# A two-layer attention trunk: the first half of layer one's output projection in pairs of tokens by 512 columns

## The chip, the cores and the metric

One core of one Trainium2 chip runs the whole kernel. The metric is the device time of one execution in microseconds (us), lower is better. Where a time is that of several runs, it is their median.

## What is computed

The trunk has two layers on 512 tokens by 1024 channels in float32. Layer one is a sparse-attention mixer of three branches (compressed, selected, sliding window), layer two a differential attention. The change lies in the last step of layer one, `o @ w_out`:

```python
    o = gate[..., 0:1] * o_c + gate[..., 1:2] * o_s + gate[..., 2:3] * o_w
    o = o.astype(u.dtype).reshape(b, s, NSA_WIDTH) * jax.nn.silu(z)
    return o @ w_out
...
        x = x + rmsnorm(y, norm_post[i])
```

`o` has 512 tokens by 1024 channels (16 heads of 64), `w_out` is 1024 by 1024.

## The kernel before

**Products.** A float32 product is made from three products of rounded parts: activations and weights are each split into a rounded value (`hi`, on ScalarE, L99) and the remainder (`lo`, on VectorE, L104), and `hi*hi`, `hi*lo` and `lo*hi` are added up in a PSUM bank. In the projection this is `mm` (L481): a 128 by 128 block of the attention output (128 channels, the k-chunk, by 128 tokens) is loaded into TensorE as the held operand, and columns of `w_out` stream past it. The attention output lies transposed in bigF (`oT`, 8 chunks of 128 channels by 512 tokens), its two parts in bigA and bigB (`U["oh"]`, `U["ol"]`). The names in the trace follow: `whi`/`wlo` are the two parts of a weight piece, `mm`, `S`, `T` and `av` are PSUM banks (two, two, three and one of them).

**Weights.** All weights of the program come as one stream of pieces (`ws`). A piece is loaded by SP's queue into one of two raw buffers (`wraw`, L125) and split by `ws.split()` into one of three pairs of buffers (`whi`, `wlo`). As a rule POOL does both parts (L170, L172). The "quick" pieces around the projection are rounded on ScalarE (L168), and their remainders go by turns to VectorE and POOL (L172). The three "extra" pieces of the second half are loaded into `P` tiles (L121), of which there are eleven and which the softmaxes use as well, and split into `wx`. A split of the next piece is asked for at the end of each piece's use; its load follows when a raw buffer is free.

**The first half of the projection** (`ojobs` with `early`). Output columns 0 to 511 are made while the attention still runs. Job oA makes columns 0 to 255 of all four tiles of 128 tokens from k-chunks 0 to 5, in the two `mm` banks, with two tokens' 256 columns in each bank. Job oB does the same for columns 256 to 511 in the two `S` banks. Each has weight pieces of 4 and 2 chunks by 256 columns. Job oC (`late_run`) adds chunks 6 and 7 to all of them when the last heads are done, and ends each tile and half with `y_evac` (L467, L468: a square sum on ScalarE, a product with the norm's weight on VectorE). Then job o1 makes columns 512 to 1023, 512 at a time, from four pieces that are all held.

**The order of the work.** The attention of the last group of heads is written as units (scores and softmax in `a`, transposes in `t`, products with V in `v`; L888 is the product with V). oA is spread over the last slots of that loop. After the loop come the remaining `t` and `v` calls, and after each of them two steps of oB (`fill`, `OB = (2,2,2)`); a step is a yield of `early_run`, three matmuls. The last unit is the compressed branch (`Cmp`): its `t` makes the transposed probabilities and the masked V (L980), its two `v` calls have three products each (L989 to L991) and add them to chunks 6 and 7 (L993). Then `fill(99)` writes out the rest of oB:

```python
    fill(99)
    for c, e in ((6, getattr(nc, ZE[0])), (7, getattr(nc, ZE[1]))):
        e.tensor_tensor(oT[:, c, :], oT[:, c, :], T["z", c], op=OP.mult)
    for c in (6, 7):
        osplit(c)
```

The multiplication by z (L1089) of chunk 6 is on POOL, of chunk 7 on VectorE; `osplit` makes the two parts. oC, o1 and the first jobs of layer two follow in an order written by hand. The rest is put in order by a scheduler that simulates a timeline; each engine then takes its instructions in the order that comes out.

Of the kernel before, what the change touches and what calls it, by code (L numbers as in the profile page):

```python
# [18 lines left out]
S = 512  # L19
# [35 lines left out]
D = 1024  # L55
NT = S // 128
# [11 lines left out]
def trunk(ctx: ExitStack, tc: tile.TileContext, x, table, npre, npost, w_in, pe_k, w1_k, w2_k,  # L68
# [11 lines left out]
    def bank(tag):  # L80
        return ps.tile([128, 512], F32, name=tag, tag=tag, bufs={"mm": 2, "S": 2, "T": 3, "av": 1}[tag])

    def slot(tag, shape, dt=F32):
        return big.tile(shape, dt, name="big" + tag, tag="big" + tag)
# [4 lines left out]
    def pttile(dt=F32R):  # L89
        return work.tile([128, 512], dt, name="PT", tag="PT", bufs=NPT)  # L90

    def small(n, dt=F32, tag="st", bufs=8):
        return work.tile([128, n], dt, name=tag, tag=tag, bufs=bufs)

    def drows(src, off, ap):
        return bass.AP(tensor=src.tensor, offset=src.offset + off, ap=ap)
# [81 lines left out]
    T = {}  # L178
    todo = []
    ws = Stream()  # L180
    U = {}

    def wcols(w, width, col, n, k0=0, nk=KD):
        return (lambda a, m: drows(w, (k0 + a) * 128 * width + col, [[width, 128], [128 * width, m], [1, n]])), nk, n
# [159 lines left out]
    def part_sum(ss, m=EPS):  # L344

        m0 = small(1, tag="m0", bufs=6)
        if isinstance(m, float):
            nc.vector.tensor_scalar(m0, ss, 1.0 / D, m, op0=OP.mult, op1=OP.add)
        else:
            nc.vector.scalar_tensor_tensor(m0, ss, 1.0 / D, m, op0=OP.mult, op1=OP.add)  # L350
        return m0
# [112 lines left out]
    def y_evac(t, p, a, n, last):  # L464
        c = slice(a, a + n)
        ss = small(1, tag="ss")
        nc.scalar.activation(pttile(F32)[:, :n], p, AF.Square, accum_out=ss)  # L467
        nc.vector.tensor_tensor(T["y"][:, t, c], p, T["gp"][a // 512][:, a % 512:a % 512 + n], op=OP.mult)  # L468
        if last:
            T["yend"](t, ss)  # L470
        else:
            T["ym", t] = part_sum(ss, T.get(("ym", t), EPS))

    def ojobs(name, w, early):


        specs = [[wcols(w, D, n * 512, 512, 2 * i, 2) for i in range(4)] for n in range(2)]

        def mm(p, t, k, wt, start, stop):
            for j, (wi, u) in enumerate(((0, "oh"), (1, "oh"), (0, "ol"))):  # L480
                nc.tensor.matmul(p, U[u][:, k, t * 128:(t + 1) * 128], wt[wi],  # L481
                                 start=start and j == 0, stop=stop and j == 2, skip_group_check=True)

        def run0(i):
            ps_ = [bank(b) for b in ("mm", "S", "mm", "S")]
            for c in range(4):
                h, l = ws.cut.pop(i + c)
                for t in range(NT):
                    for k in range(2):
                        mm(ps_[t], t, 2 * c + k, (h[:, k], l[:, k]), c == 0 and k == 0, c == 3 and k == 1)  # L490
                        yield 640.0
                    if c == 3:
                        y_evac(t, ps_[t], 0, 512, False)
                ws.split()

        def run1(i):
            for _ in range(2):
                ws.split()
            cut = [ws.cut.pop(i + c) for c in range(4)]
            for t in range(NT):  # L500
                parts = 1 if early or t < NT - 1 else 2
                n = 512 // parts
                for q in range(parts):
                    p = bank(("mm", "S")[(t + q) % 2])[:, :n]
                    for k in range(KD):
                        h, l = (v[:, k % 2, q * n:q * n + n] for v in cut[k // 2])
                        mm(p, t, k, (h, l), k == 0, k == KD - 1)
                        yield 640.0 / parts
                    y_evac(t, p, 512 + q * n, n, q == parts - 1)
            ws.split()  # L510
            ws.split()

        def early_run(q):
            def run(i):
                T["ob", q] = [bank(("mm", "S")[q]) for _ in range(2)]
                for c in range(2):
                    h, l = ws.cut.pop(i + c)
                    for k in range((4, 2)[c]):
                        if q == 0 and todo and todo[0] == 4 * c + k:
                            osplit(todo.pop(0))  # L520
                        for t in range(NT):
                            mm(T["ob", q][t // 2][:, t % 2 * 256:t % 2 * 256 + 256], t, 4 * c + k, (h[:, k], l[:, k]),
                               c == 0 and k == 0 and t % 2 == 0, False)
                            yield 320.0
                    ws.split()
            return run

        def late_run(i):
            h, l = ws.cut.pop(i)
            for t0 in (0, 2):  # L530
                for q in range(2):
                    c = slice(q * 256, q * 256 + 256)
                    for t in (t0, t0 + 1):
                        for k in range(2):
                            mm(T["ob", q][t // 2][:, t % 2 * 256:t % 2 * 256 + 256], t, 6 + k, (h[:, k, c], l[:, k, c]),
                               False, k == 1)
                            yield 320.0
                for t in (t0, t0 + 1):
                    for q in range(2):
                        y_evac(t, T["ob", q][t // 2][:, t % 2 * 256:t % 2 * 256 + 256], q * 256, 256, False)  # L540
            ws.split()

        if early:
            for q in range(2):
                Job(name + "AB"[q], [wcols(w, D, q * 256, 256, 0, 4), wcols(w, D, q * 256, 256, 4, 2)], early_run(q),
                    24 * 320.0)
            Job(name + "C", [wcols(w, D, 0, 512, 6, 2)], late_run, 16 * 320.0)
        else:
            Job(name + "0", specs[0], run0, 8 * 4 * 640.0)
        j = Job(name + "1", specs[1], run1, 8 * 4 * 640.0)  # L550
        ws.extra |= set(range(j.first + 1, j.first + 4))
        ws.quick |= set(range(j.first - (QN if early else 4), j.first + 4))
# [31 lines left out]
    for c in (4, 5, 6, 7):  # L584
        zjob(c)
    ojobs("o", w_out, True)


# [29 lines left out]
    dqk(6), dqk(7)  # L618
    dz(6), dz(7)
    ojobs("do", dw_out, False)  # L620
    index = {j.name: i for i, j in enumerate(jobs)}
    ws.extra.add(jobs[index['dv1']].first)
# [91 lines left out]
    for i, key in enumerate(("kcs", "vcs")):  # L714

        t = slot("CD"[i], [128, 5, 8, 33])
# [283 lines left out]
    def osplit(c):  # L1000
        hi(U["oh"][:, c], oT[:, c])
        lo(U["ol"][:, c], oT[:, c], U["oh"][:, c])
# [72 lines left out]
    i = 0  # L1075
# [265 lines left out]
```

## Time and profile before

| | |
|---|---|
| Runs shown, us | 646.47, 646.88, 647.7 (median 646.88) |
| Profiled execution, us | 647.41 |
| Its span, first to last instruction, us | 645.6 |
| Mean granted clock of TensorE | 0.997 |
| TensorE busy | 629.6 us, 98% of the span, 3447 matmuls |
| VectorE, ScalarE, POOL busy | 62%, 53%, 62% |
| Chain that ended last | TensorE 84%, VectorE 7%, ScalarE 4% |
| DMA | 59.94 MB, 93 GB/s over the span |

In the timelines that the prediction reads, a row is: start in us, duration in us, engine, line, operation, output <- inputs, shape, count, and in brackets the idle time of the engine just before and what ended it. Rows of TensorE have a modelled end, so the spacing is read from start to start. PEld is the loading of the held operand, SPq the issue of a DMA on SP's queue.

### The profile page before, as it was taken

The numbers are of one execution on the slowest core, as the hardware profiler recorded it, in microseconds if no ns is written. First come the engines' busy times: TensorE is split into PE (matmuls) and PEld (weight loads), VectorE is DVE, ScalarE is ACT, GpSimd is POOL, SyncE is SP. The second block draws the span as 40 slices with busy tenths as digits, with TensorE's granted clock in tenths as the row PEclk, the third lists the DMA queues.
The fourth block names the chain that finished last, engine by engine and source line by source line (L and its number), as shares of the span: only waits on it lengthen the run. The fifth ranks groups of instructions, "written<-read, shape, count | busy, mean of one in ns | idle before, by whom it ended". The sixth has DMA issues, their size and how long they took to land.

```text
span 645.6 us, 10462 instructions
## 1 busy us (share of the span) xinstructions
PE 629.6 (98%) x3447; PEld 534.1 (83%) x3447; DVE 397.4 (62%) x1142; ACT 342.7 (53%) x902; POOL 402.0 (62%) x663
## 2 busy tenths in 40 slices
PE   8999999999999999999999999999999999999996
PEld 5988888888788888888888898888888888878785
DVE  5421335678768868979777800245657767787544
ACT  7221234767667777868555410344574466677331
POOL 5558668878588596678485657865666555514200
PEclk9999999999999999999999999999999999999998
DMA  7646423214022111101953132423222322117102
GB/s 252 165 104 160 130 81 87 63 35 98 2 66 64 36 48 52 49 17 35 304 165 126 66 98 66 130 70 111 80 69 82 82 67 70 61 66 266 61 34 97
DMA packets 71915, 59.94 MB, mean 93 GB/s; under 512 B 3613, under 2 KB 62901, under 8 KB 71862
## 3 DMA queue, kind: packets, MB, share of 16 engines
q1 hardware_dynamic: 71140, 56.93, 30.2%
q10 hardware_dynamic: 722, 2.36, 0.9%
q8 instruction: 27, 0.44, 0.3%
q14 instruction: 26, 0.21, 0.1%
HBM read 54.52 MB, written 4.76 MB: 92 GB/s over the span
## 4 chain that ended last, share of the span: by engine, by line
PE 84%; DVE 7%; ACT 4%; issue 2%; DMA 1%; SPq 0%; DVEq 0%; ACTq 0%
PE mm L203 39%; PE mm L481 6%; PE av L888 5%; PE T L874 5%; PE S L226 5%; PE S L818 4%; PE S L819 4%; PE S L481 4%; PE mm L226 3%; PE T L226 2%; PE av L1224 2%; PE T L737 1%; DMA bigF<-in_x_dram 1%; PE T L1214 1%; DVE bigB L104 1%
## 5 line engine op out<-in xcount | busy, mean ns | idle before, releaser
L172 POOL TENSOR_TENSOR wlo<-wraw,whi 128x256 fp32r<-128x256 f32 (+2 forms) x239 | 183.6, 797 | 19.8 <-ACT whi L168 15.7
L170 POOL TENSOR_SCALAR whi<-wraw 128x256 fp32r<-128x256 f32 (+2 forms) x232 | 94.0, 431 | 100.9 <-PE mm L203 79.3
L812 ACT ACTIVATE P<-P,st 128x512 f32<-128x512 f32 (+3 forms) x192 | 107.3, 560 | 83.8 <-DVE st L810 82.8
L868 POOL TENSOR_SCALAR P<-P,st,gate 128x512 f32<-128x512 f32 (+2 forms) x96 | 66.6, 704 | 20.6 <-DVE st L865 17.9
L203 PE MATMUL mm<-bigF,whi 128*128 128x512 f32 x192 | 77.7, 405 | 0.1
L203 PE MATMUL mm<-bigE,whi 128*128 128x512 f32 x192 | 76.6, 399 | 0.0
L203 PE MATMUL mm<-bigA,whi 128*128 128x512 f32 x192 | 75.8, 396 | 0.1
L203 PE MATMUL mm<-bigF,wlo 128*128 128x512 f32 x192 | 75.6, 394 | 0.0
L203 PE MATMUL mm<-bigA,wlo 128*128 128x512 f32 x192 | 75.5, 393 | 0.0
L203 PE MATMUL mm<-bigB,whi 128*128 128x512 f32 x192 | 75.4, 392 | 0.0
L810 DVE CUSTOM_DVE_ANT_0 P<-S,BT 128x128 f32<-128x128 f32 (+2 forms) x144 | 59.0, 419 | 23.0 <-PE S L819 19.4
L104 DVE TENSOR_TENSOR PT<-T,PT 128x512 fp32r<-128x512 f32 x84 | 57.2, 686 | 4.3 <-PE av L888 1.8
L99 ACT ACTIVATE PT<-T 128x512 fp32r<-128x512 f32 x84 | 49.1, 594 | 13.4 <-PE T L874 8.3
L99 ACT ACTIVATE stk<-mm 64x512 fp32r<-64x512 f32 x64 | 37.9, 592 | 28.2 <-PE mm L203 17.9
L888 PE MATMUL av<-PT,bigE 128*128 128x512 f32 x144 | 52.4, 419 | 0.1
L104 DVE TENSOR_TENSOR stk<-mm,stk 64x512 fp32r<-64x512 f32 x32 | 22.1, 689 | 49.5 <-ACT stk L99 48.9
L874 PE MATMUL T<-ident,P 128*128 128x128 f32 x320 | 50.5, 272 | 0.0
L874 PEld LDWEIGHTS T<-ident,P 128*128 128x128 f32 x320 | 40.6, 140 | 11.1
L810 DVE CUSTOM_DVE_ANT_1 P<-S,BT 128x512 f32<-128x512 f32 x48 | 32.9, 689 | 24.1 <-PE S L819 20.5
L203 PEld LDWEIGHTS mm<-bigB,whi 128*128 128x128 f32 x192 | 36.1, 188 | 8.0
L203 PEld LDWEIGHTS mm<-bigE,whi 128*128 128x128 f32 x192 | 36.1, 188 | 7.7
L203 PEld LDWEIGHTS mm<-bigF,whi 128*128 128x128 f32 x192 | 36.2, 188 | 5.9 <-issue 0.5
(300 smaller groups left out, 1496.0 us busy)
## 6 DMA issues: line engine op xcount, KB each, us to landing
wraw<-in_diff_w_in_dram SPq DMA_DIRECT2D x31, 512.0 KB, 4.0
wraw<-in_nsa_w_in_dram SPq DMA_DIRECT2D x26, 512.0 KB, 3.8
BT<-rd SPq DMA_DIRECT2D x32, 128.0 KB, 3.2
wraw<-in_diff_w_out_dram SPq DMA_DIRECT2D x5, 512.0 KB, 3.9
wraw<-in_nsa_w_out_dram SPq DMA_DIRECT2D x4, 512.0 KB, 3.6
bigD<-in_x_dram SPq DMA_DIRECT2D x4, 512.0 KB, 6.8
x1d<-bigD ACTq DMA_DIRECT2D x4, 512.0 KB, 2.7
bigF<-x1d SPq DMA_DIRECT2D x4, 512.0 KB, 6.3
```

Source lines behind the costliest of these rows:

```text
L99: return nc.scalar.activation(dst, src, AF.Copy, scale=scale)
L104: return nc.vector.tensor_tensor(dst, src, h.bitcast(F32), op=OP.subtract)
L170: nc.gpsimd.tensor_scalar(h[:, a:b], v, 1.0, 0.0, op0=OP.mult, op1=OP.add)
L172: e.tensor_tensor(l[:, a:b], v, h[:, a:b].bitcast(F32), op=OP.subtract)
L203: T["mm"] = nc.tensor.matmul(p[:, a:b], wt[:, k, :], u[:, k, a:b], start=(k == 0 and j == 0), stop=(k == KD - 1 and j == 2)).ins
L226: nc.tensor.matmul(acc[t], u[:, k0 + k, t * 128:(t + 1) * 128], wt[:, k, :], start=(ci == 0 and k == 0 and j == 0 and t % per == 0), stop= ...
L481: nc.tensor.matmul(p, U[u][:, k, t * 128:(t + 1) * 128], wt[wi], start=start and j == 0, stop=stop and j == 2, skip_group_check=True)
L810: nc.vector.tensor_tensor_reduce(out=o, in0=i0, in1=b, op0=OP.add, op1=OP.min, scale=-1.0, scalar=BIG, accum_out=nm)
L812: nc.scalar.activation(pt[:, :n], pt[:, :n], AF.Exp, bias=nm, scale=-1.0, accum_out=den)
L868: NORM(nc, i, br, qb).tensor_scalar(self.P[i][:, :n], self.P[i][:, :n], st[:, 8 + i:9 + i], gate[:, NT - 1 - qb, c:c + 1], op0=OP.mult, op ...
L874: T["tmark"] = nc.tensor.transpose(p[:, j * 128:(j + 1) * 128], self.P[j][:, kb * 128:(kb + 1) * 128], ident).ins
L888: nc.tensor.matmul(av, T["V"][:, br, kb, g, :], p, start=(br == 0 and kb == 0 and j == 0), stop=(br == 1 and kb == qb and j == 1))
```

## The change

oA now makes all 512 columns of token tiles 0 and 1 from chunks 0 to 5, oB those of tiles 2 and 3. Each tile has a PSUM bank of its own (`mm` for 0 and 1, `S` for 2 and 3). Both jobs use the same three weight pieces of 2 chunks by 512 columns; oA holds them, and oB gives them up one after the other. A step is again three matmuls, now of 512 columns. oC does the same four tiles with 512 columns, and there are four `y_evac` of 512 columns in place of eight of 256. The weight stream has four pieces in place of five, and the calls of `ws.split()` move: one in oA, two in oB, one in oC. After the change the lines are two lower (L987 is what L989 was).

```diff
--- before.py
+++ after.py
@@ -512,39 +512,37 @@
 
         def early_run(q):
             def run(i):
-                T["ob", q] = [bank(("mm", "S")[q]) for _ in range(2)]
-                for c in range(2):
-                    h, l = ws.cut.pop(i + c)
-                    for k in range((4, 2)[c]):
-                        if q == 0 and todo and todo[0] == 4 * c + k:
+                for t in (2 * q, 2 * q + 1):
+                    T["ob", t] = bank(("mm", "S")[q])
+                if q == 0:
+                    T["ow"] = i
+                for c in range(3):
+                    h, l = ws.cut[T["ow"] + c]
+                    for k in range(2):
+                        if q == 0 and todo and todo[0] == 2 * c + k:
                             osplit(todo.pop(0))
-                        for t in range(NT):
-                            mm(T["ob", q][t // 2][:, t % 2 * 256:t % 2 * 256 + 256], t, 4 * c + k, (h[:, k], l[:, k]),
-                               c == 0 and k == 0 and t % 2 == 0, False)
-                            yield 320.0
-                    ws.split()
+                        for t in (2 * q, 2 * q + 1):
+                            mm(T["ob", t], t, 2 * c + k, (h[:, k], l[:, k]), c == 0 and k == 0, False)
+                            yield 640.0
+                    if q:
+                        ws.cut.pop(T["ow"] + c)
+                    if c < (1, 2)[q]:
+                        ws.split()
             return run
 
         def late_run(i):
             h, l = ws.cut.pop(i)
-            for t0 in (0, 2):
-                for q in range(2):
-                    c = slice(q * 256, q * 256 + 256)
-                    for t in (t0, t0 + 1):
-                        for k in range(2):
-                            mm(T["ob", q][t // 2][:, t % 2 * 256:t % 2 * 256 + 256], t, 6 + k, (h[:, k, c], l[:, k, c]),
-                               False, k == 1)
-                            yield 320.0
-                for t in (t0, t0 + 1):
-                    for q in range(2):
-                        y_evac(t, T["ob", q][t // 2][:, t % 2 * 256:t % 2 * 256 + 256], q * 256, 256, False)
+            for t in range(NT):
+                for k in range(2):
+                    mm(T["ob", t], t, 6 + k, (h[:, k], l[:, k]), False, k == 1)
+                    yield 640.0
+                y_evac(t, T["ob", t], 0, 512, False)
             ws.split()
 
         if early:
             for q in range(2):
-                Job(name + "AB"[q], [wcols(w, D, q * 256, 256, 0, 4), wcols(w, D, q * 256, 256, 4, 2)], early_run(q),
-                    24 * 320.0)
-            Job(name + "C", [wcols(w, D, 0, 512, 6, 2)], late_run, 16 * 320.0)
+                Job(name + "AB"[q], [] if q else specs[0][:3], early_run(q), 12 * 640.0)
+            Job(name + "C", specs[0][3:], late_run, 8 * 640.0)
         else:
             Job(name + "0", specs[0], run0, 8 * 4 * 640.0)
         j = Job(name + "1", specs[1], run1, 8 * 4 * 640.0)
```

**TensorE, around the last compressed product.** Before (`T_3928` is the last product's bank, `S_3856` and `S_3857` are oB's, `mm_3599` is the first of oC's):

```order
L481 MATMUL S_3857<-whi_3765,bigB_3586 128x256
L989 MATMUL T_3928<-PT_3884,PT_3888 128x512
L990 MATMUL T_3928<-PT_3884,PT_3888 128x512
L991 MATMUL T_3928<-PT_3885,PT_3888 128x512
L481 MATMUL S_3856<-whi_3765,bigA_3585 128x256
L481 MATMUL S_3856<-wlo_3766,bigA_3585 128x256
L481 MATMUL S_3856<-whi_3765,bigB_3586 128x256
...
L481 MATMUL S_3857<-whi_3823,bigB_3586 128x256
L481 MATMUL mm_3599<-whi_3951,bigA_3585 128x256
L481 MATMUL mm_3599<-wlo_3952,bigA_3585 128x256
```

Now (`T_3871` and `T_3888` are the two products' banks, `S_3804` and `S_3805` oB's, `mm_3595` the first of oC's):

```order
L886 MATMUL av_3772<-PT_3818,bigE_153 128x512
L987 MATMUL T_3871<-PT_3832,PT_3836 128x512
L988 MATMUL T_3871<-PT_3832,PT_3836 128x512
L989 MATMUL T_3871<-PT_3833,PT_3836 128x512
...
L481 MATMUL S_3805<-wlo_3674,bigA_3581 128x512
L481 MATMUL S_3805<-whi_3673,bigB_3582 128x512
L987 MATMUL T_3888<-PT_3832,PT_3836 128x512
L988 MATMUL T_3888<-PT_3832,PT_3836 128x512
L989 MATMUL T_3888<-PT_3833,PT_3836 128x512
L481 MATMUL mm_3595<-whi_3847,bigA_3581 128x512
L481 MATMUL mm_3595<-wlo_3848,bigA_3581 128x512
```

Before, 36 matmuls of oB (the first three and the last are shown) stand between the last product and oC. Now none does: oB's last six stand between the two products, and oC follows the last product directly.

**POOL, around the multiplication of chunk 6 by z** (`bigF_1086<-bigF_1086,zt`). Before:

```order
L172 TENSOR_TENSOR wlo_3952<-wraw_3775,whi_3951 128x512
L1089 TENSOR_TENSOR bigF_1086<-bigF_1086,zt_3404 128x512
L172 TENSOR_TENSOR wlo_3982<-wraw_3829,whi_3981 128x512
L170 TENSOR_SCALAR whi_4396<-wraw_4122 128x256 x2
L172 TENSOR_TENSOR wx_4111<-P_3832,wx_4110 128x512
L170 TENSOR_SCALAR whi_4396<-wraw_4122 128x256 x2
L172 TENSOR_TENSOR wlo_4397<-wraw_4122,whi_4396 128x256
```

Now:

```order
L172 TENSOR_TENSOR wlo_3848<-wraw_3576,whi_3847 128x512
L172 TENSOR_TENSOR wlo_3877<-wraw_3679,whi_3876 128x512
L170 TENSOR_SCALAR whi_4260<-wraw_3986 128x256 x4
L1087 TENSOR_TENSOR bigF_1086<-bigF_1086,zt_3400 128x512
L172 TENSOR_TENSOR wlo_4261<-wraw_3986,whi_4260 128x256 x4
L172 TENSOR_TENSOR wx_3975<-P_3681,wx_3974 128x512
L172 TENSOR_TENSOR wx_3981<-P_3686,wx_3980 128x512
L172 TENSOR_TENSOR wx_3989<-P_3689,wx_3988 128x512
```

The splits of layer two's first weights (`whi_4396` before, `whi_4260` now) stood behind the multiplication and now stand ahead of it. `whi_4260` takes the buffer of `whi_3673`, oB's last weight piece.

**VectorE, in the same place.** Before (`PT_3885` is the remainder of the compressed branch's probabilities, `PT_3888` its masked V):

```order
L104 TENSOR_TENSOR PT_3853<-T_3847,PT_3852 128x512
L104 TENSOR_TENSOR PT_3870<-T_3864,PT_3869 128x512
L104 TENSOR_TENSOR PT_3885<-T_3879,PT_3884 128x512
L980 SCALAR_TENSOR_TENSOR PT_3888<-vcmp_846,bmask_403,PT_3888 128x64 x4
L900 TENSOR_TENSOR bigF_1086<-av_3795,PT_3907 64x2x128 x2
L993 TENSOR_TENSOR bigF_1086<-bigF_1086,T_3917 128x512
L993 TENSOR_TENSOR bigF_1086<-bigF_1086,T_3928 128x512
L1089 TENSOR_TENSOR bigF_1086<-bigF_1086,zt_3582 128x512
L172 TENSOR_TENSOR wlo_3982<-wraw_3829,whi_3981 128x512
```

Now (`PT_3833` and `PT_3836` are those two):

```order
L104 TENSOR_TENSOR PT_3801<-T_3795,PT_3800 128x512
L104 TENSOR_TENSOR PT_3818<-T_3812,PT_3817 128x512
L172 TENSOR_TENSOR wlo_3848<-wraw_3576,whi_3847 128x512
L172 TENSOR_TENSOR wlo_3877<-wraw_3679,whi_3876 128x512
L104 TENSOR_TENSOR PT_3833<-T_3827,PT_3832 128x512
L978 SCALAR_TENSOR_TENSOR PT_3836<-vcmp_846,bmask_403,PT_3836 128x64 x4
L898 TENSOR_TENSOR bigF_1086<-av_3772,PT_3861 64x2x128 x2
L991 TENSOR_TENSOR bigF_1086<-bigF_1086,T_3871 128x512
L991 TENSOR_TENSOR bigF_1086<-bigF_1086,T_3888 128x512
L1087 TENSOR_TENSOR bigF_1086<-bigF_1086,zt_3578 128x512
```

The remainders of two weight pieces (`wlo_3848`, `wlo_3877`) now stand ahead of the compressed branch's operands; before, one of them stood some rows earlier and the other behind the multiplication by z.

## Rows read from the trace of the kernel before

**Rows 1.** The page's busy times and shares of the span.

```profile
PE 629.6 (98%) x3447; PEld 534.1 (83%) x3447; DVE 397.4 (62%) x1142; ACT 342.7 (53%) x902; POOL 402.0 (62%) x663
```

**Rows 2.** Busy time by stage: stretch, its length, engines, granted clock, DMA.

```profile
core 0: us, PE busy (x) PEld busy (x) DVE busy (x) ACT busy (x) POOL busy (x), PEclk, DMA share, GB/s
295.50:326.80 31.30, 30.40 (x223) 27.72 (x222) 26.37 (x65) 21.28 (x51) 20.66 (x24) 1.00 0.66 221
326.80:333.20 6.40, 6.21 (x50) 5.82 (x49) 5.78 (x15) 4.93 (x16) 4.81 (x7) 1.00 0.58 176
333.20:355.90 22.70, 22.70 (x104) 18.45 (x104) 16.67 (x47) 11.12 (x33) 16.18 (x20) 1.00 0.27 94
```

**Rows 3.** TensorE's waits from 295 to 345 us: total, times, longest.

```profile
PE S L818 <- DVE st L810: 0.5, 1, 0.5
PE S L818 <- DVE cp L828: 0.2, 1, 0.2
PE T L989 <- ACT PT L99: 0.2, 1, 0.2
PE mm L481 <- DVE bigB L104: 0.2, 1, 0.2
```

**Rows 4.** TensorE's timeline around the last compressed product and oC's start.

```profile
322.29 0.39 PE L991 MATMUL T<-PT 128*128 128x512 f32 x1
322.52 0.28 PE L481 MATMUL S<-whi,bigA 128*128 128x256 f32 x1
...
326.71 0.28 PE L481 MATMUL S<-whi,bigB 128*128 128x256 f32 x1
326.83 0.28 PE L481 MATMUL mm<-whi,bigA 128*128 128x256 f32 x1
...
327.41 0.39 PE L481 MATMUL mm<-whi,bigB 128*128 128x256 f32 x1 [0.19 <-DVE bigB L104]
```

**Rows 5.** The timeline of the other engines from 322 to 328 us.

```profile
322.26 1.28 DVE L993 TENSOR_TENSOR bigF<-bigF,T 128x512 f32<-128x512 f32 x2
...
323.02 1.29 POOL L1089 TENSOR_TENSOR bigF<-bigF,zt 128x512 f32<-128x512 f32 x1 [7.74 <-DVE bigF L993]
...
323.58 1.29 DVE L1089 TENSOR_TENSOR bigF<-bigF,zt 128x512 f32<-128x512 f32 x1
...
324.20 1.16 ACT L168 ACTIVATE whi<-wraw 128x512 fp32r<-128x512 f32 x2 [2.92 <-issue]
...
325.26 1.14 ACT L99 ACTIVATE bigA<-bigF 128x512 fp32r<-128x512 f32 x2
...
325.44 1.32 DVE L172 TENSOR_TENSOR wlo<-wraw,whi 128x512 fp32r<-128x512 f32 x1 [0.58 <-ACT whi L168]
...
326.68 1.28 DVE L104 TENSOR_TENSOR bigB<-bigF,bigA 128x512 fp32r<-128x512 f32 x2
```

**Rows 6.** TensorE's timeline of the second half: first matmul of its first and second tile.

```profile
333.27 0.40 PE L481 MATMUL mm<-whi,bigA 128*128 128x512 f32 x1
...
338.86 0.39 PE L481 MATMUL S<-whi,bigA 128*128 128x512 f32 x1
```

**Rows 7.** POOL's splits and the issue of the first weights of layer two.

```profile
322.26 0.38 SPq L125 DMA_DIRECT2D wraw<-in_diff_w_in_dram  x1
...
328.39 1.25 POOL L170 TENSOR_SCALAR whi<-wraw 128x256 fp32r<-128x256 f32 x2 [2.18 <-DMA wraw<-in_diff_w_in_dram]
...
337.38 1.53 POOL L170 TENSOR_SCALAR whi<-wraw 128x256 fp32r<-128x256 f32 x4
```

**Rows 8.** VectorE's timeline: a weight remainder, the probabilities' remainder, the masks.

```profile
312.53 0.69 DVE L172 TENSOR_TENSOR wlo<-wraw,whi 128x512 fp32r<-128x512 f32 x1 [0.24 <-ACT whi L168]
...
319.04 0.69 DVE L104 TENSOR_TENSOR PT<-T,PT 128x512 fp32r<-128x512 f32 x1 [0.93 <-PE av L888]
319.97 1.00 DVE L980 SCALAR_TENSOR_TENSOR PT<-vcmp,bmask,PT 128x64 fp32r<-128x64 f32 x4 [0.23 <-ACT PT L99]
```

**Rows 9.** DMA from 300 to 345 us: busy tenths in 40 slices; issues, KB, landing.

```profile
DMA  0008806486999999889999995875220000680078
...
P<-in_nsa_w_out_dram SPq DMA_DIRECT2D x6, 256.0 KB, 6.7
```

## The prediction

> **What bounds the kernel now.** I read first the busy line of the page: TensorE works 629.6 of 645.6 us [rows 1], so time is won or lost only where TensorE does less work or stands still. Next the busy times by stage [rows 2]: in the stage of the first half of the projection (295.5 to 326.8) TensorE is busy 30.40 of 31.30 us, from there to the second half 6.21 of 6.40, in the second half all of the time. So there is 0.9 us of idling to win in the stage, while anything that makes TensorE stand still adds to the span one for one. The wait table of the stretch agrees: four waits, 1.1 us in all, the longest 0.5 [rows 3]. The granted clock is 1.00 in all three stretches [rows 2], the higher of the two levels (2.4 GHz).
>
> Third, TensorE's timeline around the last two attention products [rows 4]. The last compressed-branch product starts at 322.29 and ends the attention. Then 36 matmuls of oB, 256 columns each, run from 322.52 to 326.83 without a gap, and oC, which needs channels 768 to 1023 of the attention, starts at 326.83. Beside these 4.3 us runs the chain that makes those channels [rows 5]: VectorE adds the product (0.64 us each), POOL and VectorE multiply by z (1.29), ScalarE rounds (0.57 each, delayed by two weight splits at 324.20), VectorE makes the remainders, the first from 326.68. It ends just too late: TensorE waits 0.19 us at 327.41 for the first remainder. **Those 36 matmuls are the cover of this chain**, and the change is to be judged by what becomes of it.
>
> **The change, part by part.**
>
> *Fewer, wider matmuls.* oA, oB and oC have 72 + 72 + 48 = 192 matmuls of 256 columns; the change makes them 96 of 512. Two of 256 take, by 322.52 to 326.71 (35 spacings, 0.1197 each), 0.2394 us [rows 4]; one of 512, by the second half's 333.27 to 338.86 (24 spacings), 0.2329 [rows 6]. The saving is 0.0065 x 96 = 0.6 us, 0.47 of it ahead of oC. The rate is seen on the same operands, so I give it no range. The Trainium skill ("TensorE: Matmul & The Clock Gate", section "Wait — 56ns, not 53.3ns?") has N / 2.4 GHz + 2.5 ns from start to start on a warm array; by that, 109.2 and 215.7 ns, the saving would be an estimated 0.25 us. Both spacings in the trace are longer than this rule's, so the rows decide.
>
> *Evacuations.* oC's eight evacuations of 256 columns become four of 512. ScalarE and VectorE do less, but no wait in the stretch names them [rows 3]: zero, hidden beside oC's matmuls.
>
> *The cover is gone.* In the new order no matmul of oB is left behind the last product: the next one is oC's first. All of oB stands ahead of the product, six of its matmuls between the two products, as before. TensorE's work up to oC is the same less the saving, so it would come to oC at 326.83 - 0.47 = 326.36, plus what it waits on the way, and oC cannot go on until the chain has run.
>
> *The chain is longer.* On POOL the z-multiply of channels 768 to 895 now stands behind four splits of layer two's first weights. Those write the third weight buffer, which oB's last matmul reads, and oB's last matmul stands three products ahead of TensorE's end: 3 x 0.233 = 0.7 us. From the end of oB: four splits 1.53 [rows 7], z-multiply 1.29 [rows 5], ScalarE 0.57 [rows 5], three handoffs of about 0.1 (POOL started 0.12 after the add that it needed: 322.90 to 323.02 [rows 5]), together 3.7 us, of which 0.7 lies beside the products. So TensorE stands still for 3.0 us. For the next operand, the remainder, VectorE needs 0.64 [rows 5] while two matmuls take 0.47, so 0.2 more, as much as the idling in oC before. The bounds: were the splits over before the multiply is wanted, the chain would be add, multiply and rounding, 0.64 + 1.29 + 0.57 + 0.3 = 2.8 from the end of the first product, of which 2.1 lies under six oB matmuls and the second product (9 x 0.233): a stall of 0.7, or some 1.3 if VectorE's multiply of the other half (channels 896 to 1023) decides. Were the weights late, the stall is longer; that is a rival below. I take 3.0, since the splits are ahead in POOL's queue.
>
> *Added waits ahead of it.* (1) On VectorE, the remainder of the last product's operand and its four masks now stand behind a weight remainder that waits for ScalarE's split, and this for oB's second weight piece. Behind that piece 22 TensorE instructions of 0.233 are left, 5.1 us, so its buffer is free at about 326.36 - 5.1 = 321.2. Then follow ScalarE's 1.16 and VectorE's 1.32 [rows 5], the operand's remainder 0.69 and the masks 1.00 [rows 8]: 325.4 at the latest. With half of ScalarE's split and the 0.69 that VectorE took for such a remainder at 312.53 [rows 8] it is 324.2. TensorE wants the first of them at 326.36 - 11 x 0.233 = 323.8. So the wait is 0.4 to 1.6; I take the middle, 1.0, since rows of both lengths stand in this stretch. (2) Four softmaxes of the last attention unit move some ten places back on VectorE, behind tiles that now hold raw weights. Below, nothing: TensorE has oA's matmuls to run. Above, the longest wait for VectorE in the stretch, 0.46 [rows 3], once more. I take the upper value, since VectorE is busy 26.37 of 31.30 us in the stage [rows 2].
>
> *Later transfers.* The raw weights of the second half are loaded ahead of the bias and the residual on SP's queue. Six of 256 KB land 6.7 us after issue there, in a stretch where the DMA engines are at 80 to 99% [rows 9]. I cost it at nothing, because the residual is read only by the second half's first end, at 339 [rows 6]; if that cover is gone, it is the rival below.
>
> **The sum**, against the profiled execution (647.41 us, span 645.6):
> oC starts at 326.36 + 1.0 + 0.5 (added waits) + 3.0 (stall) = 330.9, in place of 326.83. oC takes 24 x 0.233 + 0.2 = 5.8 in place of 6.44, so the second half starts at 336.7 in place of 333.27: +3.4 us. From there both kernels do the same on TensorE, which is busy 22.70 of 22.70 us in the second half [rows 2]. 647.41 + 3.4 = 650.8; the median of the runs shown, 646.88, lies 0.5 below the profiled one, so **650.3 us**. With the low bounds of the waits (0.4 and 0) it is +2.3, with the high ones (1.6 and 0.5) +4.0, and with a stall half a microsecond off either way +1.8 to +4.5: 648.7 to 651.4.
>
> **Rivals.**
> *Stall mostly hidden.* The splits run on POOL before the multiply is wanted, or the multiply goes ahead of them; then the stall is 0.7 to 1.3 and the waits ahead of it 0 to 0.5: -0.6 + 0.7 to 1.3 + 0 to 0.5, or +0.1 to +1.2: 647.0 to 648.1. For it: POOL idled 7.74 us before this multiply in the kernel before [rows 5], so it has time. Against it: the buffer that the splits write is read until the end of oB, whatever POOL's free time is. On whether the multiply can go first, no row tells. The Trainium skill ("Perfetto Trace Analysis", section "Tensor Engine Instruction (MATMUL, LD_WEIGHTS)") says that GpSimd, like ScalarE and VectorE, takes its instructions strictly in order; by this rule it can't, and by an engine that reorders, the time would be that of this rival.
>
> *Faster.* The oB matmuls that stand earlier fill what TensorE idled: the 0.9 us of the stage [rows 2]; with the 0.6 of the wider matmuls that is -1.5, or 645.4. It decides if the new chain costs less than 0.2 us, so that the last product and the multiply are done some 3 us earlier than I find. For it: TensorE has as much work ready earlier. Against it: the waits of the stage are for VectorE, which gets no less to do ahead of 322, and oC cannot start without the chain.
>
> *Weights of layer two late.* Their transfer starts when the raw buffer is free, that is once the split of oC's weights is done on both POOL and VectorE, and before it came 2.18 us too late for POOL as it was: issued at 322.26, landed at 328.39 [rows 7]. If it lands 1 to 2.5 us after the end of oB, the multiply behind it waits as long: +4.4 to +5.9, or 651.3 to 652.8. For it: 6.1 us in flight at a full queue. Against it: six tiles of other weights are now loaded earlier, so the queue may be shorter.
>
> That the change does not do what it says I give no chance, since the new order has the 96 matmuls of 512.
>
> **How the numbers follow.** What a measurement can tell from no change is about 0.2%, 1.3 us: below 645.6 is faster, above 648.2 slower. The forecast gets 0.60, the hidden stall 0.16, late weights 0.14, faster 0.10. The hidden stall lies within 0.2% nearly whole (0.14 of its 0.16); forecast and late weights are slower (0.74), with the other 0.02. So: faster 0.10, same 0.14, slower 0.76. The range leaves out the faster case and the top of the late weights, and starts with the hidden stall: 646.9 to 652.4.
>
> **What would show it.** Right: after the last compressed product TensorE's timeline has a gap of 2.5 to 3.5 us, put down to ScalarE or POOL (the multiply); on POOL's timeline four splits of layer two stand right ahead of the multiply; within the products, a wait of about 1 us for the masks or the operand's remainder; spacings of 0.233 in oA, oB and oC; the second half starts 1.8 to 4.5 us later than at 333.27, and the rest is shifted by the same. Wrong: a gap below 1.3 us there; or a gap whose splits wait for the DMA; or idling of more than 1 us ahead of 318, which none of my terms has; or a shift that layer two takes back.

## The result and the profile after

The change makes the kernel slower: 654.09 us (median of 4 runs, 653.86 to 655.38) where the kernel before took 647.22 (4 runs) beside it. The ratio is 1.0105, 95% interval [1.0093, 1.0117]: +6.8 us. The forecast was 650.3, the range ended at 652.4, so the sign was right and the size about half.

The wait table of TensorE, from 290 to 350 us of the changed kernel (answers to [rows 3]; total, times, longest):

```profile
PE mm L481 <- ACT bigA L99: 5.3, 1, 5.3
PE mm L481 <- DVE zt L452: 0.6, 1, 0.6
PE S L816 <- DVE st L808: 0.3, 1, 0.3
PE T L987 <- ACT PT L99: 0.2, 1, 0.2
```

Nearly all of it is one wait of 5.3 us. TensorE's timeline shows where (answers to [rows 4]): the last compressed product starts at 327.24, and oC at 332.90 instead of right behind 0.23 us later. No matmul of oB is left in between.

```profile
326.79 0.39 PE L987 MATMUL T<-PT 128*128 128x512 f32 x1
327.02 0.39 PE L988 MATMUL T<-PT 128*128 128x512 f32 x1
327.24 0.39 PE L989 MATMUL T<-PT 128*128 128x512 f32 x1
332.90 0.79 PE L481 MATMUL mm<-whi,bigA 128*128 128x512 f32 x1 [5.26 <-ACT bigA L99]
...
335.18 0.63 PE L481 MATMUL mm<-wlo,bigA 128*128 128x512 f32 x1
335.61 0.63 PE L481 MATMUL mm<-whi,bigB 128*128 128x512 f32 x1
336.03 0.63 PE L481 MATMUL mm<-whi,bigA 128*128 128x512 f32 x1
...
337.01 0.39 PE L481 MATMUL mm<-whi,bigA 128*128 128x512 f32 x1
...
340.42 0.39 PE L481 MATMUL mm<-whi,bigA 128*128 128x512 f32 x1
```

The chain of waits in the same stretch (start, length, what) tells who held it. Read from top to bottom: VectorE's remainder of oC's weights frees the raw buffer, the weights of layer two are in flight for 6.94 us, POOL splits them for 1.95, and only then does POOL multiply chunk 6 by z, ScalarE round it and VectorE make the remainder.

```profile
320.48 1.37 DVE wlo L172
...
321.91 6.94 DMA wraw<-in_diff_w_in_dram
...
329.01 1.95 POOL whi L170 x4
330.96 1.23 POOL bigF L1087
...
332.21 0.64 ACT bigA L99
...
332.88 1.24 DVE bigB L104
...
334.16 3.70 PE mm L481 x10
```

Busy times by stage (columns as in [rows 2]; the last stretch begins with the second half of the projection) show the second price: TensorE comes out of the wait at a granted clock of 0.50, the lower of its two levels (1.2 GHz), and stays there until about 336.5.

```profile
327.50:332.90 5.40, 0.14 (x2) 0.01 (x1) 2.32 (x4) 1.31 (x3) 3.89 (x7) 0.71 0.16 53
332.90:336.50 3.60, 3.56 (x8) 2.35 (x9) 3.60 (x4) 3.30 (x7) 3.60 (x4) 0.50 0.05 13
336.50:340.40 3.90, 3.90 (x18) 3.25 (x17) 3.35 (x6) 1.83 (x6) 3.90 (x3) 0.98 0.69 211
340.40:363.10 22.70, 22.70 (x103) 18.48 (x102) 15.58 (x45) 10.47 (x29) 12.18 (x16) 1.00 0.20 73
```

In that time the spacing of 512 columns is 0.43 us (335.18 to 336.03), against 0.23 later. The second half starts at 340.42, where it was 333.27 [rows 6]: +7.15. Some 0.5 of this lies further ahead, since the same score matmul (L816, before L818) starts at 299.42 in this execution and at 298.96 in that of before. Of the other 6.7, oC's later start makes 5.6: the wait of 5.3 and one of 0.6 for `zt` near 301, less 0.2 that the kernel before waited there for `cp` [rows 3]. The remaining 1.1 is oC itself, which takes 7.52 us in place of 6.44. Not all of the slow matmuls' extra time is lost, since the third of them had to wait for VectorE's remainder in any case (334.16 behind 332.88 + 1.24 in the chain above). Layer two gives 0.8 back: a wait of TensorE for VectorE's `stk` (L435), 0.83 us at 572.98 in the kernel before, is gone; why is not shown.

### The profile page after: what moved, and what is told of

Read it like the earlier page. It is cut to its first block, busy times and chain, and to the rows that moved or that the text cites. A ratio compares the mean times of both kernels' runs of the same rounds, so it can differ in the third digit from the quotient of the medians.

```text
span 652.1 us, 10242 instructions
## 1 busy us (share of the span) xinstructions
PE 630.4 (97%) x3351; PEld 530.3 (81%) x3351; DVE 398.0 (61%) x1134; ACT 341.1 (52%) x894; POOL 399.2 (61%) x651
## 4 chain that ended last, share of the span: by engine, by line
PE 84%; DVE 8%; DMA 3%; issue 2%; ACT 2%; POOL 1%; SPq 0%; DVEq 0%; ACTq 0%; POOLq 0%
PE mm L203 40%; PE mm L481 5%; PE S L226 5%; PE T L872 5%; PE av L886 5%; PE S L816 4%; PE S L817 4%; PE S L481 3%; PE mm L226 3%; PE av L1222 2%; PE T L226 2%; DMA wraw<-in_diff_w_in_dram 2%; PE T L735 1%; DMA bigF<-in_x_dram 1%; DVE bigB L104 1%
## 5 line engine op out<-in xcount | busy, mean ns | idle before, releaser
L170 POOL TENSOR_SCALAR whi<-wraw 128x256 fp32r<-128x256 f32 (+2 forms) x226 | 92.5, 434 | 103.2 <-PE mm L203 79.8
```

The lines of the kernel that those rows point to most:

```text
L170: nc.gpsimd.tensor_scalar(h[:, a:b], v, 1.0, 0.0, op0=OP.mult, op1=OP.add)
```

## The experiments

Theory: oB's matmuls no longer cover the chain from the last product to oC, and the chain is held on POOL by splits that wait for late weights; coming out of the wait, TensorE runs slowly for a while. Main rival: the new tiling itself costs, through its earlier transfers and moved softmaxes.

**1. One step of oB per call.** A step is now twice as long, so two steps after each remaining attention call use oB up. This run takes one:

```diff
-OB = (2,2,2)
+OB = (1,1,1)
```

> The change with one step of oB after each remaining attention call instead of two, so that 6 of its 12 steps (18 matmuls of 512, 4.1 us) stand behind the last compressed product again; on POOL the multiplication by z then stands ahead of layer two's splits. Theory (lost cover, with the multiplication behind late splits): the gap ahead of oC shrinks from 5.3 to under 0.6 us, no slow clock, oC starts near 327.5, and the time is 646.0 to 647.5, at or just below the kernel before. Rival (the new tiling itself, through earlier transfers and moved softmaxes, delays the stage): time stays at 649 or more, with waits ahead of the last product.

Measured: 646.54 us, ratio 0.9991 [0.9982, 1.0000]. The order then has 18 matmuls of oB behind the last product, and on POOL the multiplication ahead of layer two's splits. In its timeline POOL multiplies at 324.14, and the weights, late as before, now hold nobody:

```profile
324.14 1.29 POOL L1087 TENSOR_TENSOR bigF<-bigF,zt 128x512 f32<-128x512 f32 x1 [2.96 <-DMA bigD<-in_x_dram]
...
328.93 2.06 POOL L170 TENSOR_SCALAR whi<-wraw 128x256 fp32r<-128x256 f32 x3 [0.96 <-DMA wraw<-in_diff_w_in_dram]
```

TensorE waits for nothing from 322.17 until layer two (357.76), oC starts at 327.97, the clock is 1.00 throughout. The whole loss is thus in what stands where at the end of the layer, and the tiling itself costs nothing; the main rival falls. The 0.6 us below the kernel before is at the edge of noise and is not won in this stage: the second half starts 34.4 us behind the score matmul (299.31 to 333.69), before 34.3. In layer two the wait of 0.83 us for `stk` is gone here too.

**2. Both multiplications by z on VectorE.** Here oB is still used up, but the chain no longer passes through POOL.

```diff
-ZE = 'gpsimd', 'vector'
+ZE = 'vector', 'vector'
```

> The change with both multiplications by z on VectorE; the cover stays gone. Theory (POOL's splits, which wait for the DMA, hold the chain): the multiplication follows its add at once, oC starts at about 328.7 after a gap of 1.0 to 1.5 us plus some 0.5 us of waits inside oC, the clock stays at its higher level, time 647.8 to 649.0. Rival (the missing cover alone is the cost, whichever engine multiplies): gap of 3 us or more and time 651 or more.

Measured: 649.79 us, ratio 1.0047 [1.0031, 1.0062]. At the place in question it went as expected, with waits of 0.99 and 0.73 us and a clock of 1.00. The rest that puts it above the expectation comes later: at the start of layer two TensorE waits 1.97 us for VectorE (`bigC`, L383), where the kernel before waited 0.30 at that line. VectorE has one multiplication more to do in this stretch; whether that is the reason was not tried apart.

```profile
327.32 0.50 PE L481 MATMUL mm<-whi,bigA 128*128 128x512 f32 x1 [0.99 <-ACT bigA L99]
328.79 0.50 PE L481 MATMUL mm<-whi,bigB 128*128 128x512 f32 x1 [0.73 <-DVE bigB L104]
...
359.60 1.18 PE L394 MATMUL T<-ident,bigC 128*128 128x128 f32 x8 [1.97 <-DVE bigC L383]
```

**3. Throwaway matmuls in the gap.** They read chunk 0 and write a bank that nobody reads:

```diff
+        keep = bank("T")
+        with tc.issue_after(T["tmark"]):
+            for _ in range(22):
+                nc.tensor.matmul(keep, U["oh"][:, 0, 0:128], U["oh"][:, 0, :], start=True, stop=True, ...)
         run.upto("oC")
```

> The change with 22 throwaway matmuls of 512 columns (into a bank that nobody reads) between the last product and oC. Theory (the gap costs its 5.3 us and then 1.7 us more, because TensorE came out of it at the lower clock): oC starts at 332.9 as in the change, but its spacing is 0.23 from the first matmul on, time 652.0 to 652.8. Rival (the slow spacing in oC comes from something else, such as operands that arrive late): oC as slow as before and time 653.6 to 654.5.

Measured: 652.07 us, ratio 1.0074 [1.0058, 1.0089], 2.0 us below the change by the ratios. oC starts as late as before behind the last product (326.69 to 332.31), and the clock is 1.00 in oC:

```profile
326.91 5.15 PE L1142 MATMUL T<-bigA 128*128 128x512 f32 x22
...
332.31 0.50 PE L481 MATMUL mm<-whi,bigA 128*128 128x512 f32 x1 [0.25 <-ACT bigA L99]
...
333.59 0.50 PE L481 MATMUL mm<-whi,bigB 128*128 128x512 f32 x1 [0.54 <-DVE bigB L104]
...
338.71 0.39 PE L481 MATMUL mm<-whi,bigA 128*128 128x512 f32 x1
```

So the lower clock follows from the wait. Its price is read from oC: TensorE, now faster, waits 0.54 us in it for VectorE's remainder, and oC takes 6.40 us (332.31 to 338.71) where the change took 7.52. That is 1.1 us. The rest of the 2.0 is not the clock's: in the traces 0.6 lies ahead (the score matmul starts at 298.85, in the change at 299.42), and two sets of runs of one order differ by more than what is left (sixth experiment).

**4. The kernel before without its cover.**

```diff
-OB = (2,2,2)
+OB = (4,4,4)
```

> The kernel before (256 columns, all tokens) with four steps of oB after each remaining call, so that no oB matmul is left behind the last product; on POOL one weight remainder, but no split of layer two, comes ahead of the multiplication. Theory (cover): a gap of 1.5 to 2.5 us ahead of oC and 648.5 to 650.0. Rival (the cover does not matter, only the new tiling): 647.2 as before.

Measured: 652.18 us, ratio 1.0072 [1.0057, 1.0088], more than expected. With 256 columns, all tokens and its own transfers, the kernel before loses most of what the change loses once no oB matmul stands behind the last product. Its trace (650.86 us, the fastest of its runs) has waits of 1.33, 0.56 and 0.18 us ahead of and in oC and a clock of 0.71 and 0.83 in the two stretches from 327.5 to 335.0. Reckoned from the same score matmul (L818, 297.99 here, 298.96 before), the second half starts 3.7 us later (335.97, before 333.27), and L394 waits 0.6 longer: 4.3 of the 4.9 us between the medians. Of the 3.7, 1.6 is oC's later start and 2.0 is oC itself (8.49 us, before 6.44), with two waits for VectorE's remainder and the lower clock.

```profile
327.48 0.39 PE L481 MATMUL mm<-whi,bigA 128*128 128x256 f32 x1 [1.33 <-ACT bigA L99]
...
328.53 0.39 PE L481 MATMUL mm<-whi,bigB 128*128 128x256 f32 x1 [0.56 <-DVE bigB L104]
```

**5. POOL's order alone put back.** The first splits of layer two may not be issued before the multiplication of chunk 6 (`T["z6"]`, set where it is made); on the other engines nothing moves ahead of oC's start:

```diff
+            if "z6" in T and self.ncut == jobs[index["dv0"]].first:
+                with tc.issue_after(T["z6"]):
+                    return self.split_now()
...
```

> The change with one thing put back: layer two's first splits may not be issued on POOL before the multiplication by z of chunk 6. The cover stays gone, the products and all other engines' orders are those of the change. Theory (the multiplication is held by the splits): it starts right behind its add, near 327.2, oC at about 329.2 after a gap of 1.7 us instead of 5.3; time 649.0 to 651.0, the upper end if TensorE still falls to its lower clock for a while. Rival (something else holds the chain): oC at 331 or later, 653 or more.

Measured: 648.35 us where the kernel before took 647.67 on the same chip, ratio 1.0014 [1.0004, 1.0025]. That is better than expected, since the clock did not fall: it is 1.00 in all stretches. POOL multiplies at 325.93, and the wait is 1.61:

```profile
325.93 1.27 POOL L1093 TENSOR_TENSOR bigF<-bigF,zt 128x512 f32<-128x512 f32 x1 [2.73 <-DVE bigF L997]
...
327.62 2.84 POOL L176 TENSOR_SCALAR whi<-wraw 128x256 fp32r<-128x256 f32 x4 [0.42 <-DMA wraw<-in_diff_w_in_dram]
...
327.91 0.50 PE L487 MATMUL mm<-whi,bigA 128*128 128x512 f32 x1 [1.61 <-ACT bigA L99]
```

Reckoned from the score matmul (297.98), layer two's first wait (L394) comes 1.6 us later than in the kernel before (358.28 against 357.64), and layer two gives 0.8 of that back. One place in POOL's queue is worth 0.9% of the 1.05% (0.7% against the sixth experiment, the order of the change once more, on the same chip). Against the first experiment, which has the cover too, what is left is the price of the lost cover when POOL's order is right: 0.23%, 1.5 us, little more than two sets of runs of one order differ by (sixth experiment). In the fourth, where the clock fell, losing the cover cost 4.7 us by the ratio.

**6. The residual's loads held back, first try.**

```diff
-        for t in range(NT):
-            nc.sync.dma_start(xr[:, t, :], ...)
+        with tc.issue_after(T["tmark"]):
+            for t in range(NT):
+                nc.sync.dma_start(xr[:, t, :], ...)
```

> The change with the loads of the residual (4 of 512 KB) held back until the last compressed product, so that layer two's first weights have the DMA queue to themselves; the splits stay ahead of the multiplication. Theory (2.2 us of the gap are the late weights, late because the queue is full of loads issued earlier): the weights land 4 to 5 us after their issue, the splits start at the end of oB, near 326.8, oC 2 us or more earlier than in the change, time 651.4 to 652.4 (lower if the clock then stays up). Rival (they are late by their own 7 us in flight): no change, 653.6 to 654.5.

Measured: 653.01 us, ratio 1.0086 [1.0073, 1.0099], wait 5.87 us. It tells nothing on the theory: SP issued these loads between 313.46 and 317.41, as in the change (314.15 to 317.57). In the traces every engine and queue has the instructions of the change in the order of the change, so this is the change measured a second time, 1.0086 beside 1.0105. The loss is thus 5.6 to 6.8 us, and two ratios that lie 0.2% apart can't be told apart here.

**7. The residual's loads on ScalarE's queue.** Behind ScalarE's rounding of the last chunks (`T["o7"]`) they can't go early:

```diff
...
-            nc.sync.dma_start(xr[:, t, :], ...)
...
+                with tc.issue_after(T["o7"]):
+                    nc.scalar.dma_start(xr[:, t, :], ...)
```

> The change with the residual's loads issued by ScalarE's queue behind its rounding of the last chunks (the try to hold them back on SP's queue left them where they were). Orders on POOL, VectorE and TensorE are those of the change. Theory (2.2 us of the gap are weights that share the queue with the residual): they land 4 to 5 us after their issue near 321.5, the splits start near 326.8 at the end of oB, the gap is 3 us instead of 5.3, ratio 1.006 to 1.008 in place of 1.0105, less still if the clock stays up. Rival (late on their own): gap and time as in the change.

Measured: 651.13 us, ratio 1.0061 [1.0046, 1.0077]. The weights land 3.6 to 3.8 us after their issue (5.6 to 6.9 in the change), the splits now wait for TensorE's last read of the buffer and not for the DMA, and the wait is 3.31 us. The chain of waits of this run, as that of the change above:

```profile
324.62 1.40 PE S L481 x6
...
326.10 1.51 POOL whi L170 x4
327.62 1.67 POOL bigF L1087
...
329.31 0.64 ACT bigA L99
...
329.97 1.01 DVE bigB L104
```

So 2 us of the wait were weights late behind the residual's loads. TensorE still fell to its lower clock (spacing 0.43 from 331.61 to 334.17), and oC took 7.71 us. The second half starts 39.3 us behind the score matmul, 1.7 less than in the change; by the ratios the time fell by 2.8 us, against the sixth experiment by 1.6.

**8 to 10. Toward a better version.** All three have one step of oB per call. The first (the eighth experiment) also moves oA's start by a slot (`ODELAY = 1`), the second holds back the residual's loads as in the sixth, the third lets oA take both chunks of a piece for its first token tile before the second:

```diff
-                    for k in range(2):
+                    for t, k in ((0, 0), (0, 1), (1, 0), (1, 1)) if q == 0 else ((2, 0), (3, 0), (2, 1), (3, 1)):
...
-                        for t in (2 * q, 2 * q + 1):
...
```

> The first experiment (one step of oB after each call) with oA starting one slot later, so that the bank that it takes has been emptied: its wait of 0.57 us for VectorE near 301 should go. If that wait is on the path, 645.8 to 646.3; if other work just waits in its place, 646.5 as the first experiment.

> The first experiment with the residual's loads held back until the last product. With the cover in place the weights' landing hides behind oB and oC, so no change: 646.2 to 646.9; it would be slower (647 or more) if the residual then comes late for the first end of the second half.

> The first experiment with oA taking both chunks of a piece for its first token tile before it turns to the second, so that the second bank, which VectorE empties late, is wanted some 0.7 us later. The wait of 0.57 us near 301 should go or shrink below 0.1; if it is on the path, the ratio to before falls from 0.9991 to about 0.998 (some 646.0 where before is 647.2); if other waits grow in its place it stays at 0.999.

Measured: the later start is worse, 1.0016 [1.0007, 1.0025]: the bank that oA takes is emptied even later behind VectorE's other work, and the wait for `zt` is 1.78 us in place of 0.57. Behind this wait TensorE fell to its lower clock here too:

```profile
303.00:304.00 1.00, 1.00 (x4) 0.86 (x4) 0.99 (x6) 0.50 (x3) 0.40 (x1) 0.50 1.00 340
304.00:306.00 2.00, 2.00 (x7) 1.66 (x6) 1.97 (x5) 0.71 (x3) 1.76 (x4) 0.52 0.49 184
```

The second is the first experiment over again, since the loads did not move there either (313.76 to 317.49) and every order is the same: 0.9987 [0.9978, 0.9996]. In the third the wait for `zt` is gone and another of 0.58 us (for `cp`, L825) has come 2.5 us later: 0.9990 [0.9982, 0.9999]. So two kernels with the cover, one of them measured twice, lie at 0.999, below the change and by a hair below the kernel before, and neither of these two orders of oA wins the wait near 301.

## Why the prediction was right and wrong

*Right.* **What bounds the kernel** and **the cover**: giving the 18 matmuls back returns all of the loss. **The chain is longer**: the multiplication started right behind the splits (330.93 behind 329.01 + 1.95), and putting it ahead took 0.7 to 0.9% away. On the rule of strict order that the prediction weighed ("Perfetto Trace Analysis", section "Tensor Engine Instruction (MATMUL, LD_WEIGHTS)" of the Trainium skill), the trace agrees: the multiplication's input was ready at 327.18 and POOL, idle for 4.48 us until 329.01, did not take it before the splits. With weights in time (the seventh experiment) the wait was 3.31 us, where the sum had 3.0. oC then started 3.7 us later, reckoned from the score matmul (298.40 to 329.99, before 298.96 to 326.83), where the sum had 4.1; that these meet is in part luck, since only 0.3 of the 1.5 us of added waits came, and of the 0.5 saved nothing shows (below). So the stall of the forecast case is sized rightly, but it is not the case that the change makes.

*Wrong: "Later transfers ... I cost it at nothing".* The cover that was named, the late use of the residual, was there for the residual alone. What had none was the transfer behind it in the same queue, layer two's first weights. The prediction had the number: 6.1 us in flight for them, from 322.26 [rows 7]; 322.26 + 6.1 = 328.4 is later than the 327.2 at which the sum let the splits start. It also misread what held that issue in the kernel before. It let the load start once oC's weights are split; but their last split had ended by 315.3 (POOL then idles 7.74 us until 323.02 [rows 5]), and SP's waits from 321 to 323 us name a load of the residual:

```profile
SPq L125 <- DMA bigD<-in_x_dram: 0.9, 1, 0.9
```

So the row told of a queue that was full already. The case stood among the rivals with 0.14, on the argument that six other loads come earlier. Measured in the change: issued at 321.91, 6.94 us in flight, splits 2.2 us after oB's end (326.79 to 329.01), 1.95 in place of 1.53 for them; the prediction's own sign of being wrong, a gap whose splits wait for the DMA, is there. The rival's sum with 2.2 gives +5.6; the 6.7 in the trace lies 1.1 above it.

*Wrong: a term that was missing.* No sum, the rival's either, had the clock after a wait of several microseconds. Measured: 1.1 us, oC's 7.52 in the change against 6.40 in the third experiment. The kernel before has no such wait in this stage, so its rows do not price this; that slow matmuls could follow a long wait should have widened the range upward. The Trainium skill ("TensorE: Matmul & The Clock Gate", section "Wait — 56ns, not 53.3ns?") gives 426.7 ns from start to start for 512 columns on a cold array. The trace agrees: 0.43 us.

*Mis-sized.* **The sum's oC**: 5.8 us were taken, with 0.2 of waiting; at a clock of 1.00 it took 6.40 (third experiment), with 0.54 of waiting for VectorE's remainder. **The bound without splits in the way**: a stall of 0.7 to 1.3 was named, the fifth experiment had 1.61. **Added waits**: the wait for the masks (1.0 taken) did not come: in the changed kernel's timeline no wait stands ahead of L988. In its place came one of 0.56 us for `zt` near 301, because oA's second bank is now wanted before VectorE has emptied it; it was not foreseen. **Fewer, wider matmuls**: 512 columns took 0.226 to 0.228 us in oB and oC of the changed kernel (14 spacings from 319.09 to 322.26, 15 from 337.01 to 340.42), less than the 0.2329 of [rows 6], so the saving in these stretches is 0.012 to 0.013 a matmul and not 0.0065. But it does not show ahead of oC: from the score matmul to oC's start, waits taken off, both kernels take 27.4 us. The saving is not measured alone.

## What to carry to other kernels

Work that covers a wait at the end of a stage is often counted in steps: when a step is made longer, count how much work is left behind the last product that the next stage waits for. When a scheduler reorders the program, look on each queue at what now stands ahead of the one operation that the stage's end waits for; ask for its inputs' arrival too, issue plus time in flight, and put that beside the time at which the sum needs them. A wait of TensorE costs its length, and the matmuls after it may take nearly twice as long until the clock is back.

## What the runs showed that was not expected

The length of a wait alone did not decide whether TensorE came back slowly. After 1.61 us (fifth experiment) and after 0.99 and 0.73 (second) the granted clock stayed at 1.00; after 1.33 us, followed by 0.56 and 0.18, it fell (fourth experiment: 0.71 in the stretch from 327.5 to 331.2), and after 1.78 (eighth), 3.31 and 5.26 it fell too. What tells the fourth from the fifth was not tried. And a spacing of TensorE is no constant of the program: in the changed kernel alone, 512 columns took 0.2325 us from 318.16 to 319.09 and 0.2264 right behind, to 322.26, in the same job oB; the second half took 0.2317 (24 spacings from 340.42), before 0.2329 [rows 6]. The granted clock was 1.00 in all of these; the cause is open.
